# Two of six pairs of an encoder's down projection as seven block products, with corrections added to x by DMA

## The chip, the cores and the metric

The kernel runs on one core of a Trainium2 chip. The metric is the device time of one execution in microseconds (us), the median of several runs. A core has five engines, each with its own queue of instructions that it works through in order, and waits on semaphores: TensorE (PE in the profile), VectorE (DVE), ScalarE (ACT), GpSimd (POOL) and SyncE (SP), which here only issues loads. Sixteen DMA engines carry the transfers that SP and POOL issue.

## The reference

A trunk of two layers over 256 tokens of width 2048, all in float32. In each layer, with RMSNorm h = norm(x):

```python
proj = einsum('bsd,de->bse', h, w_in[l])          # q, k, v and a gated branch uv
a = dilated_attention(rope(q), rope(k), v)        # 8 heads of 128
g = chunked_spatial_gating(uv, ...)
x = x + einsum('bse,ed->bsd', concat(norm(a), norm(g)), w_out[l])
h = norm(x)
ff = silu(einsum(h, w_gate[l])) * einsum(h, w_up[l])   # 5632 columns
x = x + einsum('bsf,fd->bsd', ff, w_down[l])           # "down", 5632 rows to 2048 columns
```

A last RMSNorm follows. The change is in the last line, and in attention's tables (cosines, sines, mask).

## The kernel before

**Products.** A float32 product is made of three TensorE products (TERMS): each operand is split into a high part, which ScalarE rounds with a copy, and a low part, which VectorE gets by subtraction (`put_split2` for activations, `Group.split`, lines 861 and 862, for weights). high x high, high x low and low x high are summed in a PSUM bank.

**Groups.** The work is a row of 28 groups per layer. A group computes 256 tokens by two blocks of 512 columns, in four banks: v and z are the two blocks for the first 128 tokens, x and w for the second. The groups are, in order: 0 v, 1 and 2 qk (queries and keys), 3 gv, 4 u, 5 to 8 the output projection; then ff and down in four parts (FF_PARTS 3, 3, 3, 2): ff 9 to 11, down0 12 and 13, ff 14 to 16, down1 17 and 18, ff 19 to 21, down2 22 and 23, ff 24 and 25, down3 26 and 27. Layer 1 repeats them with numbers 28 higher. One ff group makes one block of 512 ff columns; a part's first down group adds the part's ff blocks, times their rows of w_down, to columns 0 to 1023 of x, its second to the rest.

**Pairs and slots.** The contraction goes by pairs of 128-row tiles. A plain pair is a slot "N" twice, once per half of the tokens, with 24 matmuls in all. In ff groups four of eight pairs already run as seven block products M1 to M7 (Strassen's scheme in Winograd's form), one slot each, in the order ORDER (FIRST for a layer's first). Their weights come as four quarters q11, q12, q22, q21. VectorE adds quarters in place (line 837), two further additions between quarters are accumulating DMAs from POOL's queue (line 841), and M1, M5, M6 and M7 leave corrections (lines 917 to 929) that VectorE adds to the banks at the end (line 937). Their activations need seven combinations for each pair (`sums`). Down groups before are plain: 6 pairs (4 in down3), 144 matmuls.

**Order.** The code is written slot by slot, and each engine takes its instructions in that order. Ahead of a slot's matmuls stand the loads due 5 slots later and the splits due 3 slots later (2 from an ff part's second group on); behind them one or two steps of side tasks (`spawn`, `run_side`): transposes, norms, gates, attention. `Ffn.turn` is such a task: it transposes a finished ff block in two steps (k = 0 and 2) and splits it. Loads need one of N_BIG buffers of 128x2048 ("big"), small tiles of 128x512 one of a ring of N_SX (`sx`), whose next user waits for the last user of the same buffer.

**Down's end.** When a bank of a down group closes, VectorE adds it to x in place (line 761).

## Time and profile before

| | us |
|---|---|
| median of three runs | 2159.31 (2158.47 to 2159.74) |
| profiled execution | 2160.09 |
| its span, first to last instruction | 2158.3 |
| TensorE busy | 2100.5, 9432 matmuls |
| VectorE busy | 1525.8 |
| ScalarE busy | 1072.7 |
| POOL busy | 117.7 |

The engines work beside each other, so busy times don't add up. The 1.8 us between span and execution lie around the instructions. In timelines each row has its start, its length and its count, and in square brackets the idle time of the engine ahead of it and who ended it.

### The profile page before, as it was taken

To read this page: it belongs to the slowest core of one execution; us is meant where nothing else is said; L and a number is where in the kernel's file an instruction comes from. 1 tells how busy PE (TensorE), PEld (TensorE's weight loads), DVE (VectorE), ACT (ScalarE), POOL (GpSimd) and SP (SyncE) were. 2 spreads that over 40 slices of the span, in tenths; PEclk is the share of its full clock that TensorE was granted. 3 is DMA by queue.
4 is the path that set the end of the run, shared out by engine and by line. 5 is a ranking of instruction groups with operands and counts; after the bars stand their busy time and mean duration, and the time that the engine had idled before them with its cause. 6 is when DMAs were issued, how large, how long until landed. Compare 5 with 4: busy or idle time off the path is not lost.

```text
span 2158.3 us, 23529 instructions
## 1 busy us (share of the span) xinstructions
PE 2100.5 (97%) x9432; PEld 1725.6 (80%) x9432; DVE 1525.8 (71%) x1388; ACT 1072.7 (50%) x1153; POOL 117.7 (5%) x108
## 2 busy tenths in 40 slices
PE   8999999999999999999999999999999999999997
PEld 7888887788888878888788788877888788788885
DVE  5577656886687588668655766668847875886684
ACT  6445545554455355445553555455534553554453
POOL 0220000000000000000002200000000000000000
PEclk9999999999999999999999999999999999999999
DMA  8444554676776667667544355556766665776772
GB/s 339 175 145 171 186 204 158 213 249 223 241 243 195 234 214 232 216 222 262 198 178 174 127 189 185 195 160 237 235 241 226 215 234 196 228 251 224 241 244 78
DMA packets 65134, 451.96 MB, mean 209 GB/s; under 512 B 7296, under 2 KB 7296, under 8 KB 11264
## 3 DMA queue, kind: packets, MB, share of 16 engines
q1 hardware_dynamic: 58688, 404.31, 50.1%
q0 software_dynamic: 6336, 46.14, 10.9%
q8 instruction: 74, 1.21, 0.2%
q14 instruction: 36, 0.29, 0.0%
HBM read 402.19 MB, written 2.10 MB: 187 GB/s over the span
## 4 chain that ended last, share of the span: by engine, by line
PE 50%; DVE 5%; issue 2%; ACT 2%; DMA 1%; DVEq 0%; POOLq 0%; POOL 0%; ACTq 0%
PE mm_v L884 12%; PE mm_z L884 11%; PE mm_x L884 11%; PE mm_w L884 10%; PE mm L884 5%; DVE lo_M L862 2%; DMA raw_q<-raw_q 1%; ACT hi_M L861 1%; DVE lo L862 1%; PE tpf L265 1%; DVE hl L862 0%; PE sp L449 0%; PE tpn_n L265 0%; DVE m L937 0%; PE op L489 0%
## 5 line engine op out<-in xcount | busy, mean ns | idle before, releaser
L862 DVE TENSOR_TENSOR hl<-raw,hl 128x1024 fp32r<-128x1024 f32 (+1 forms) x402 | 478.9, 1240 | 65.3 <-ACT hl L861 63.5
L861 ACT ACTIVATE hl<-raw 128x1024 fp32r<-128x1024 f32 (+1 forms) x402 | 399.6, 1048 | 129.2 <-PE mm_w L884 80.7
L862 DVE TENSOR_TENSOR lo_M<-raw_q,hi_M 128x2048 fp32r<-128x2048 f32 x154 | 348.8, 2287 | 77.3 <-ACT hi_M L861 72.5
L861 ACT ACTIVATE hi_M<-raw_q 128x2048 fp32r<-128x2048 f32 x154 | 287.3, 1910 | 108.2 <-DMA raw_q<-raw_q 82.6
L884 PE MATMUL mm<-hi_M,h_n 128*128 128x512 f32 x704 | 235.5, 395 | 8.2 <-ACT h_n L255 4.1
L862 DVE TENSOR_TENSOR lo<-raw,hi 128x2048 fp32r<-128x2048 f32 x88 | 201.1, 2285 | 41.9 <-ACT hi L861 31.5
L861 ACT ACTIVATE hi<-raw 128x2048 fp32r<-128x2048 f32 x88 | 167.1, 1907 | 54.4 <-PE mm_w L884 43.0
L884 PEld LDWEIGHTS mm<-hi_M,h_n 128*128 128x128 f32 x704 | 132.7, 189 | 38.0 <-DVE h_n L257 6.4
L884 PE MATMUL mm_v<-hl,ff 128*128 128x512 f32 x528 | 136.3, 392 | 2.7 <-ACT ff L234 2.7
L884 PE MATMUL mm<-lo_M,h_n 128*128 128x512 f32 x352 | 138.0, 392 | 0.0
L884 PE MATMUL mm_x<-hl,ff 128*128 128x512 f32 x528 | 134.9, 391 | 0.0
L884 PE MATMUL mm_z<-hl,ff 128*128 128x512 f32 x528 | 134.1, 389 | 0.0
L884 PE MATMUL mm_w<-hl,ff 128*128 128x512 f32 x528 | 134.1, 389 | 0.0
L884 PE MATMUL mm_v<-hi,hb_n 128*128 128x512 f32 x352 | 126.2, 399 | 0.0
L884 PE MATMUL mm_z<-hi,hb_n 128*128 128x512 f32 x352 | 124.3, 394 | 0.0
L884 PE MATMUL mm_x<-hi,hb_n 128*128 128x512 f32 x352 | 122.9, 390 | 0.0
L884 PE MATMUL mm_w<-hi,hb_n 128*128 128x512 f32 x352 | 122.7, 389 | 0.0
L884 PE MATMUL mm_v<-hl,h_n 128*128 128x512 f32 x420 | 113.7, 402 | 9.1 <-DVE hl L862 4.6
L884 PEld LDWEIGHTS mm_v<-hl,ff 128*128 128x128 f32 x528 | 98.0, 188 | 25.0 <-ACT ff L234 3.7
L884 PEld LDWEIGHTS mm_z<-hl,ff 128*128 128x128 f32 x528 | 99.1, 188 | 20.7
L884 PEld LDWEIGHTS mm_w<-hl,ff 128*128 128x128 f32 x528 | 99.1, 188 | 20.7
L884 PEld LDWEIGHTS mm_x<-hl,ff 128*128 128x128 f32 x528 | 98.5, 188 | 20.1
(207 smaller groups left out, 3368.4 us busy)
## 6 DMA issues: line engine op xcount, KB each, us to landing
raw<-in_w SPq DMA_DIRECT2D x287, 1024.0 KB, 4.9
raw_q<-in_w SPq DMA_DIRECT2D x88, 1024.0 KB, 6.8
raw_q<-raw_q POOLq DMA_DIRECT2D x44, 1024.0 KB, 7.8
xt<-in_x SPq DMA_DIRECT2D x4, 512.0 KB, 13.6
out<-xt SPq DMA_DIRECT2D x8, 256.0 KB, 3.1
...
raw<-in_w SPq DMA_DIRECT2D x4, 256.0 KB, 5.7
...
```

The lines of the kernel that those rows point to most:

```text
L265: nc.tensor.transpose(ps[:, j, t, :], src[:, t, (k + j) * P:(k + j + 1) * P], ident)
L861: nc.scalar.activation(out=hi[:, sl], in_=src[:, sl], func=AF.Copy)
L862: nc.vector.tensor_tensor(out=lo[:, sl], in0=src[:, sl], in1=hi[:, sl].bitcast(F32), op=ALU.subtract)
L884: nc.tensor.matmul(bank[0], lhsT=lhsT, rhs=rhs, start=bank[1], stop=stop)
```

## The change

Three things change.

**Products.** The down groups of parts 0 to 2 (twelve groups in both layers) run their first two pairs, which are the part's first ff block, as M1 to M7 in the order DOWN. The quarters come two to a buffer, `q11q12` and `q22q21`, each as one load of 1 MB; each product's high and low parts share one buffer. Per group VectorE adds quarters twice (128x1024, line 900 after) and POOL's queue twice (512 KB, line 903).

**Corrections.** ScalarE copies banks 1 and 5, VectorE makes the corrections (lines 1002, 1004, 1008, 1009 after), and `to_x` adds them to x with four accumulating DMAs of 256 KB from POOL's queue (line 989): v after M1, z after M6, x and w after M7. VectorE then adds the banks to x as before (line 816), and waits for those DMAs, because both write the same tile of x.

**Fast blocks.** For ff blocks 0, 3 and 6 `Ffn.turn` no longer splits after each transpose. ScalarE copies the transposed tiles into a raw buffer, and `sums` makes the seven combinations of both pairs and splits them.

**Tables.** The attention tables, their mask and a sum leave the constant pool for a big buffer `cm` that a Mixer takes at its start and frees after attention; layer 1 loads them a second time. N_BIG goes from 17 to 18, N_SX from 8 to 7.

The core of the diff; left out are renamed uses of the tables, the selection of the pairs and the layout of the packed weights, which follows the order of the loads.

```diff
-FAST = {"ff": 4}
+FAST = {"ff": 4, **{f"down{i}": 2 for i, n in enumerate(FF_PARTS) if n == 3}}
...
 ORDER = ("N", "M1", "N", "M5", "M2", "N", "M6", "M3", "M7", "M4", "N")
+DOWN = ("M1", "N", "M5", "N", "M2", "M6", "N", "M3", "M7", "M4", "N")
...
 LOADS = {"M1": ("q11", "q12"), "M5": ("q22",), "M2": ("q21",)}
+LOADS2 = {"M1": ("q11q12",), "M5": ("q22q21",)}
 CH = 4 * NB
-N_BIG = 17
-N_SX = 8
+N_BIG = 18
+N_SX = 7
...
 )
+FAST_BLOCKS = [sum(FF_PARTS[:i]) for i in range(len(FF_PARTS)) if FAST.get(f"down{i}")]
...
             for m in range(2):
-                yield (l, f"down{i}", m, j0 * NB, 2 * nj, 0,
+                yield (l, f"down{i}", m, j0 * NB, 2 * nj, FAST.get(f"down{i}", 0),
...
             j0 += nj
-def _order(idx, pairs, fast):
+def _order(what, idx, pairs, fast):
...
         return pairs * ("N",)
+    if what != "ff":
+        return DOWN
     return ORDER if idx else FIRST
+def _first(what, pairs, fast):
+    return pairs - fast if what == "ff" else 0
...
     colt = cpool.tile([P, DEPTH * (GC + NG)], F32, name="colt")
-    cst = cpool.tile([P, 2, NT, HD], F32, name="cst")
-    mskt = cpool.tile([P, NT, SEQ], F32, name="mskt")
...
         nc.vector.tensor_tensor(out=lo, in0=src, in1=hi.bitcast(F32), op=ALU.subtract)
-    def sums(raw, n, dst):
+    def sums(raw, n, dsts):
...
         src = r[:, :, 0:7, :].rearrange("p j f q -> p j (f q)")
-        hi, lo = (dst.rearrange("p (j h z) -> p j h z", h=2, z=7 * P)[:, :, i] for i in range(2))
-        nc.scalar.activation(out=hi, in_=src, func=AF.Copy)
+        per = n // len(dsts)
+        parts = []
+        for i, dst in enumerate(dsts):
+            z = dst.rearrange("p (j h z) -> p j h z", h=2, z=7 * P)
+            parts.append((z[:, :, 0], z[:, :, 1], src[:, i * per:(i + 1) * per]))
+        for hi, _, of in parts:
+            nc.scalar.activation(out=hi, in_=of, func=AF.Copy)
         yield 1
-        nc.vector.tensor_tensor(out=lo, in0=src, in1=hi.bitcast(F32), op=ALU.subtract)
+        for hi, lo, of in parts:
+            nc.vector.tensor_tensor(out=lo, in0=of, in1=hi.bitcast(F32), op=ALU.subtract)
...
             self.ra = self.rg = None
-            self.s2 = s2p.tile([P, SEQ], F32, tag="s2a", name=f"s2a_{l}", bufs=1)
+            self.cm = Big(f"cm_{l}")
+            self.cst = self.cm.t[:, :NB].rearrange("p (i t d) -> p i t d", i=2, t=NT)
+            self.mskt = self.cm.t[:, NB:2 * NB]
+            self.s2 = self.cm.t[:, 2 * NB:2 * NB + SEQ]
+            nc.sync.dma_start(out=self.cst, in_=cs)
+            nc.sync.dma_start(out=self.mskt, in_=msk.rearrange("p t k -> p (t k)"))
...
                     )
+                self.cm.free()
...
     class Ffn:
         def __init__(self, l, norm):
             self.l, self.norm = l, norm
-            self.blocks = {}
+            self.blocks, self.pairs = {}, {}
...
         def turn(self, m, ff, own):
-            self.blocks[m] = KTiles(f"ff_{self.l}_{m}")
+            fast = m in FAST_BLOCKS
+            if not fast:
+                self.blocks[m] = KTiles(f"ff_{self.l}_{m}")
+            else:
+                raw = Big(f"fr_{self.l}_{m}")
+                r = raw.view("p (j f q) -> p j f q", j=2, f=8)
...
                         own[0].free()
-                put_split2(self.blocks[m], k, ps.rearrange("p j t q -> p j (t q)"))
+                if fast:
+                    nc.scalar.activation(out=r[:, k // 2, 0:8:7, :], in_=ps[:, 0], func=AF.Copy)
+                    nc.scalar.activation(out=r[:, k // 2, 1:3, :], in_=ps[:, 1], func=AF.Copy)
+                else:
+                    put_split2(self.blocks[m], k, ps.rearrange("p j t q -> p j (t q)"))
+            if fast:
+                pair = [Big(f"ff_{self.l}_{m}_{i}", F32R) for i in range(2)]
+                yield from sums(raw, 2, [b.t[:, :14 * P] for b in pair])
+                self.pairs[m] = pair
+        def free(self, m):
+            for b in self.pairs[m] if m in FAST_BLOCKS else [self.blocks[m]]:
+                b.free()
+        def form(self, p):
+            m = p // 2
+            force(lambda: m in self.pairs)
+            v = self.pairs[m][p % 2].t[:, :14 * P].rearrange("p (h f q) -> p h f q", h=2, f=7)
+            return lambda hl, f: v[:, hl, FORMS[f], :]
...
     def before(l, what, idx):
         nonlocal final
-        if what == "v":
+        if what == "v" and l:
...
         return norms["n1", l].normal(p)
+    def form(l, what, p):
+        if what == "ff":
+            return norms["n2", l].form(p)
+        return ffns[l].form(sum(FF_PARTS[:int(what[4:])]) * 2 + p)
...
                 return [slot[0]]
-            return [slot[1]] if self.fast else [(slot[1], kk) for kk in range(2)]
+            return [slot[1]] if self.fast and not self.small else [(slot[1], kk) for kk in range(2)]
...
                 else:
-                    for q in LOADS.get(slot[0], ()):
-                        yield q, self.fast * NB, i
+                    for q in (LOADS2 if self.small else LOADS).get(slot[0], ()):
+                        yield q, 2 * NB * len(q) // 3 if self.small else self.fast * NB, i
...
             self.raw[key] = b
+        def block(self, q):
+            for key, b in self.raw.items():
+                if b.t is not None and isinstance(key, str) and q in key:
+                    c = key.index(q) // 3 * self.fast * NB
+                    return b.t[:, c:c + self.fast * NB]
         def add(self, to, of):
-            cols = self.fast * NB
-            a, b = (self.raw[q].t[:, :cols] for q in (to, of))
-            nc.vector.tensor_tensor(out=a, in0=a, in1=b, op=ALU.add)
+            nc.vector.tensor_tensor(out=self.block(to), in0=self.block(to), in1=self.block(of), op=ALU.add)
         def add_dma(self, to, of):
-            cols = self.fast * NB
-            nc.gpsimd.dma_start(out=self.raw[to].t[:, :cols], in_=self.raw[of].t[:, :cols], accum_op=ALU.add)
+            nc.gpsimd.dma_start(out=self.block(to), in_=self.block(of), accum_op=ALU.add)
         def need(self, key):
-            return 1 if isinstance(key, tuple) else 2
+            return 1 if isinstance(key, tuple) or self.small else 2
...
                 q = {"M1": "q11", "M5": "q11", "M6": "q11", "M2": "q21", "M4": "q21", "M7": "q12", "M3": "q22"}
-                raw, cols = self.raw[q.get(key, key)], self.fast * NB if key in PRODUCT else CH
-                src = raw.t[:, :cols]
-                own = [Big(f"{z}_{self.g}_{key}", F32R) for z in ("hi", "lo")]
-                hi, lo = (z.t[:, :cols] for z in own)
+                if key in PRODUCT:
+                    src, cols = self.block(q[key]), self.fast * NB
+                    raw = next(b for z, b in self.raw.items() if isinstance(z, str) and q[key] in z)
+                else:
+                    raw, cols = self.raw[key], CH
+                    src = raw.t
+                if self.small:
+                    own = [Big(f"hl_{self.g}_{key}", F32R)]
+                    hi, lo = own[0].t[:, :cols], own[0].t[:, cols:]
+                else:
+                    own = [Big(f"{z}_{self.g}_{key}", F32R) for z in ("hi", "lo")]
+                    hi, lo = (z.t[:, :cols] for z in own)
...
                 self.add_dma("q21", "q11")
+            elif self.small and key in ("M6", "M3"):
+                pass
...
                 for p in range(self.fast):
-                    act = norms["n2", self.l].form(self.n - self.fast + p)
+                    act = form(self.l, self.what, self.fasts[p])
...
                         z.free()
+        def to_x(self, b):
+            if self.what != "ff":
+                t, n = next(k for k, v in BANK.items() if v == b)
+                nc.gpsimd.dma_start(out=xt[2 * self.idx + n][:, t, :], in_=self.copies[b], accum_op=ALU.add)
...
                     c["v"] = c[b]
+                    self.to_x("v")
...
                 nc.vector.tensor_tensor(out=c["z"], in0=c["5"], in1=c["x"], op=ALU.subtract)
+                self.to_x("z")
...
                 c["w"] = c["5"]
+                self.to_x("x")
+                self.to_x("w")
                 return
-            if self.fast and b == "w" and "w" not in c:
+            if self.what == "ff" and b == "w" and "w" not in c:
...
                 return
-            if b in c:
+            if b in c and self.what == "ff":
...
         nc.sync.dma_start(out=xt[b], in_=x[:, :, b * NB:(b + 1) * NB])
-    nc.sync.dma_start(out=cst, in_=cs)
-    nc.sync.dma_start(out=mskt, in_=msk)
+    mixers[0] = Mixer(0, norms["n1", 0])
...
```

**Down to ff.** VectorE before, at the end of down0's second group (13) and the start of ff group 14; `hl` and `lo` are the low parts of weights, `xt` is x, `mm` a bank:

```order
L862 TENSOR_TENSOR hl_13_5_0_3884<-raw_13_5_3850,hl_13_5_0_3884 128x1024
L862 TENSOR_TENSOR hl_13_5_1_3887<-raw_13_5_3850,hl_13_5_1_3887 128x1024
L862 TENSOR_TENSOR lo_14_0_3933<-raw_14_0_3882,hi_14_0_3932 128x2048
L761 TENSOR_TENSOR xt_2_99<-mm_13_v_3770,xt_2_99 128x512
L761 TENSOR_TENSOR xt_3_100<-mm_13_z_3771,xt_3_100 128x512
L761 TENSOR_TENSOR xt_2_99<-mm_13_x_3792,xt_2_99 128x512
L761 TENSOR_TENSOR xt_3_100<-mm_13_w_3793,xt_3_100 128x512
```

The same place after the change:

```order
L932 TENSOR_TENSOR hl_13_M4_3952<-raw_13_q22q21_3761,hl_13_M4_3952 128x1024
L932 TENSOR_TENSOR hl_13_5_0_3961<-raw_13_5_3918,hl_13_5_0_3961 128x1024
L932 TENSOR_TENSOR hl_13_5_1_3964<-raw_13_5_3918,hl_13_5_1_3964 128x1024
L1008 TENSOR_TENSOR m16_13_3913<-mm_13_7_3967,m16_13_3913 128x512
L1009 TENSOR_TENSOR m5_13_3861<-m5_13_3861,m16_13_3913 128x512
L932 TENSOR_TENSOR lo_14_0_3991<-raw_14_0_3950,hi_14_0_3990 128x2048
L816 TENSOR_TENSOR xt_2_99<-mm_13_v_3818,xt_2_99 128x512
L816 TENSOR_TENSOR xt_3_100<-mm_13_z_3819,xt_3_100 128x512
L816 TENSOR_TENSOR xt_2_99<-mm_13_x_3838,xt_2_99 128x512
L816 TENSOR_TENSOR xt_3_100<-mm_13_w_3839,xt_3_100 128x512
L932 TENSOR_TENSOR lo_14_M1_4025<-raw_14_q11_3978,hi_14_M1_4024 128x2048
L900 TENSOR_TENSOR raw_14_q11_3978<-raw_14_q11_3978,raw_14_q12_3980 128x2048
```

POOL's queue after, for group 13 (before, it held nothing between groups 11 and 14):

```order
L989 DMA xt_2_99<-m1_13_3810 128x512
L903 DMA raw_13_q11q12_3728<-raw_13_q22q21_3761 128x1024
L903 DMA raw_13_q22q21_3761<-raw_13_q11q12_3728 128x1024
L989 DMA xt_3_100<-m5_16_13_3915 128x512
L989 DMA xt_2_99<-m16_13_3913 128x512
L989 DMA xt_3_100<-m5_13_3861 128x512
```

VectorE's additions to x stay ahead of the split of M1; ahead of them now stand three product splits and two bank operations, and on POOL's queue the DMAs on which the additions wait.

**The turn.** ScalarE before, in ff group 15, where ff block 3 is turned; `tpf` is the transposed tile, `m5` the copy of bank 5:

```order
L234 ACTIVATE ff_0_3_4313<-tpf_0_3_0_4331 128x2x256
L861 ACTIVATE hi_15_2_4338<-raw_15_2_4278 128x2048
L917 ACTIVATE m5_15_4355<-mm_15_5_4342 128x512
L234 ACTIVATE ff_0_3_4313<-tpf_0_3_2_4357 128x2x256
L861 ACTIVATE hi_15_M6_4376<-raw_15_q11_4180 128x2048
```

ScalarE after, `fr` being the raw buffer:

```order
L675 ACTIVATE fr_0_3_4371<-tpf_0_3_0_4389 128x2x128
L676 ACTIVATE fr_0_3_4371<-tpf_0_3_0_4389 128x256
L931 ACTIVATE hi_15_2_4396<-raw_15_2_4336 128x2048
L995 ACTIVATE m5_15_4413<-mm_15_5_4400 128x512
L675 ACTIVATE fr_0_3_4371<-tpf_0_3_2_4415 128x2x128
L676 ACTIVATE fr_0_3_4371<-tpf_0_3_2_4415 128x256
L274 ACTIVATE ff_0_3_0_4422<-fr_0_3_4371 128x896
L274 ACTIVATE ff_0_3_1_4423<-fr_0_3_4371 128x896
L931 ACTIVATE hi_15_M6_4444<-raw_15_q11_4238 128x2048
```

VectorE before, at the same place:

```order
L235 TENSOR_TENSOR ff_0_3_4313<-tpf_0_3_0_4331,ff_0_3_4313 128x2x256
L862 TENSOR_TENSOR lo_15_2_4339<-raw_15_2_4278,hi_15_2_4338 128x2048
L235 TENSOR_TENSOR ff_0_3_4313<-tpf_0_3_2_4357,ff_0_3_4313 128x2x256
L862 TENSOR_TENSOR lo_15_M6_4377<-raw_15_q11_4180,hi_15_M6_4376 128x2048
L862 TENSOR_TENSOR lo_15_M3_4395<-raw_15_q22_4237,hi_15_M3_4394 128x2048
```

VectorE after:

```order
L932 TENSOR_TENSOR lo_15_2_4397<-raw_15_2_4336,hi_15_2_4396 128x2048
L266 TENSOR_TENSOR fr_0_3_4371<-fr_0_3_4371 128x2x128 x4
L277 TENSOR_TENSOR ff_0_3_0_4422<-fr_0_3_4371,ff_0_3_0_4422 128x896
L277 TENSOR_TENSOR ff_0_3_1_4423<-fr_0_3_4371,ff_0_3_1_4423 128x896
L932 TENSOR_TENSOR lo_15_M6_4445<-raw_15_q11_4238,hi_15_M6_4444 128x2048
```

The four sums and the two splits of the block now stand together between the second N pair's low part and M6's, and M6's high part stands behind two copies more on ScalarE.

**From qk to gv.** VectorE before, in layer 0, with the engines it waits for in brackets; `rb` is one half of the rotation (POOL makes the other, `ra`), `hl_3_1` and `hl_3_2` are gv's weights:

```order
L862 TENSOR_TENSOR hl_3_1_1_1133<-raw_3_1_1064,hl_3_1_1_1133 128x1024 [waits Activation_49]
L419 TENSOR_TENSOR rb_q_0_1_1_1169<-s_q_0_1_1_1142,cst_102 128x4x64 [waits Activation_49,Pool_49]
L419 TENSOR_TENSOR rb_q_0_1_1_1169<-s_q_0_1_1_1142,cst_102 128x4x64
L419 TENSOR_TENSOR rb_k_0_1_1_1174<-s_k_0_1_1_1150,cst_102 128x4x64 [waits DVE_49,Activation_49,Pool_49]
L419 TENSOR_TENSOR rb_k_0_1_1_1174<-s_k_0_1_1_1150,cst_102 128x4x64
L862 TENSOR_TENSOR hl_3_2_0_1180<-raw_3_2_1128,hl_3_2_0_1180 128x1024 [waits DMAHW1_49,Activation_49]
L862 TENSOR_TENSOR hl_3_2_1_1183<-raw_3_2_1128,hl_3_2_1_1183 128x1024 [waits PE_49,Activation_49]
```

After:

```order
L932 TENSOR_TENSOR hl_3_1_1_1131<-raw_3_1_1062,hl_3_1_1_1131 128x1024 [waits Activation_49]
L445 TENSOR_TENSOR rb_q_0_1_1_1167<-s_q_0_1_1_1140,cm_0_128 128x4x64 [waits PE_49,Activation_49]
L445 TENSOR_TENSOR rb_q_0_1_1_1167<-s_q_0_1_1_1140,cm_0_128 128x4x64
L445 TENSOR_TENSOR rb_k_0_1_1_1172<-s_k_0_1_1_1148,cm_0_128 128x4x64 [waits DVE_49,Activation_49,Pool_49]
L445 TENSOR_TENSOR rb_k_0_1_1_1172<-s_k_0_1_1_1148,cm_0_128 128x4x64
L932 TENSOR_TENSOR hl_3_2_0_1178<-raw_3_2_1126,hl_3_2_0_1178 128x1024 [waits DMAHW1_49,Activation_49]
L932 TENSOR_TENSOR hl_3_2_1_1181<-raw_3_2_1126,hl_3_2_1_1181 128x1024 [waits Activation_49]
```

The order is the same; the second `rb_q` waits for PE in place of Pool.

## Rows read from the trace of the kernel before

**Rows 1.** Page: busy time by engine, and the granted clock by slice.

```profile
PE 2100.5 (97%) x9432; PEld 1725.6 (80%) x9432; DVE 1525.8 (71%) x1388; ACT 1072.7 (50%) x1153; POOL 117.7 (5%) x108
...
PEclk9999999999999999999999999999999999999999
```

**Rows 2.** TensorE's timeline, down2's first group: start us, us, engine, line, operation.

```profile
878.85 1.52 PE L884 MATMUL mm_v<-hl,ff 128*128 128x512 f32 x6
880.21 1.52 PE L884 MATMUL mm_z<-hl,ff 128*128 128x512 f32 x6
```

**Rows 3.** Stretches from:to: busy PE, PEld, DVE, ACT, POOL; granted clock; DMA share; GB/s.

```profile
878.85:912.20 33.35, 33.35 (x152) 27.62 (x151) 20.21 (x21) 16.35 (x18) 0.00 (x0) 1.00 0.53 190
912.20:945.07 32.87, 32.87 (x146) 27.21 (x145) 15.50 (x15) 11.90 (x9) 0.00 (x0) 1.00 0.66 256
996.00:1040.00 44.00, 43.75 (x197) 36.24 (x198) 37.33 (x30) 25.49 (x22) 0.86 (x1) 1.00 0.78 241
```

**Rows 4.** Groups by line and shape, VectorE, then ScalarE: count, busy us, mean ns.

```profile
L862 DVE TENSOR_TENSOR hl<-raw,hl 128x1024 fp32r<-128x1024 f32 x398 | 476.3, 1245 | 62.4 <-ACT hl L861 60.7
...
L837 DVE TENSOR_TENSOR raw_q<-raw_q,raw_q 128x2048 f32<-128x2048 f32 x44 | 100.9, 2292 | 1.5
...
L252 DVE TENSOR_TENSOR hr_n<-hr_n 128x256 f32<-128x256 f32 x16 | 6.1, 421 | 4.0 <-ACT hr_n L329 3.9
...
L861 ACT ACTIVATE hl<-raw 128x1024 fp32r<-128x1024 f32 x398 | 397.0, 1053 | 126.4 <-PE mm_w L884 80.7 <-DMA raw<-in_w 36.4 <-DVE hl L862 8.3
...
L917 ACT ACTIVATE m<-mm 128x512 f32<-128x512 f32 x44 | 26.3, 598 | 165.0 <-PE mm L884 165.0
```

**Rows 5.** Page: software queue and transfers, us to landing; L841: issue ns, landing us.

```profile
q0 software_dynamic: 6336, 46.14, 10.9%
...
out<-xt SPq DMA_DIRECT2D x8, 256.0 KB, 3.1
...
L841 POOL DMA_DIRECT2D raw_q<-raw_q x44: 852/862/1045, 358.3 to 2073.5; - x44
...
DMA to landing us min/median/max: 6.9/7.8/12.9
```

**Rows 6.** VectorE, then TensorE, from down2's last bank into the next ff group.

```profile
945.27 0.69 DVE L761 TENSOR_TENSOR xt<-mm_w,xt 128x512 f32<-128x512 f32 x1 [0.67 <-PE mm_w L884]
...
950.41 2.28 DVE L862 TENSOR_TENSOR lo<-raw,hi 128x2048 fp32r<-128x2048 f32 x1
...
953.46 0.39 PE L884 MATMUL mm_v<-lo,hb_n 128*128 128x512 f32 x1
```

**Rows 7.** ScalarE, VectorE, TensorE in ff group 15, at the second transpose.

```profile
617.50 5.53 ACT L861 ACTIVATE hi_M<-raw_q 128x2048 fp32r<-128x2048 f32 x3
...
616.81 2.28 DVE L862 TENSOR_TENSOR lo<-raw,hi 128x2048 fp32r<-128x2048 f32 x1
...
619.61 6.68 DVE L862 TENSOR_TENSOR lo_M<-raw_q,hi_M 128x2048 fp32r<-128x2048 f32 x3
...
616.33 0.60 PE L265 MATMUL tpf<-ident,ffn 128*128 128x128 f32 x4
...
625.18 0.39 PE L884 MATMUL mm<-lo_M,h_n 128*128 128x512 f32 x1
```

**Rows 8.** VectorE, then TensorE, from the second qk group into gv, layer 0.

```profile
154.99 1.85 DVE L419 TENSOR_TENSOR rb_q<-s_q,cst 128x256 f32<-128x256 f32 x2
159.58 0.76 DVE L419 TENSOR_TENSOR rb_k<-s_k,cst 128x256 f32<-128x256 f32 x2 [2.74 <-POOL ra_q L421]
160.26 3.44 DVE L862 TENSOR_TENSOR hl<-raw,hl 128x1024 fp32r<-128x1024 f32 x2
...
153.83 0.60 PE L430 MATMUL tpr_q<-ident,ra_q 128*128 128x128 f32 x4
...
161.53 0.97 PE L884 MATMUL mm_v<-hl,h_n 128*128 128x512 f32 x3 [0.97 <-DVE hl L862]
163.76 1.00 PE L884 MATMUL mm_v<-hl,h_n 128*128 128x512 f32 x2 [1.26 <-DVE hl L862]
```

More of the change, by code (lines that the diff above doesn't have):

```diff
@@ L333, in block @@
             if fast:
-                yield from sums(raw, len(fast), self.hs[:, (fast[0] - self.slow) * 14 * P:(fast[-1] + 1 - self.slow) * 14 * P])
+                sl = slice((fast[0] - self.slow) * 14 * P, (fast[-1] + 1 - self.slow) * 14 * P)
+                yield from sums(raw, len(fast), [self.hs[:, sl]])
                 for p in fast:
@@ L729, in after @@
             for j in range(sum(FF_PARTS[:i]), sum(FF_PARTS[:i + 1])):
-                ffns[l].blocks[j].free()
+                ffns[l].free(j)
     def normal(l, what, p):
@@ L783, in __init__ @@
             self.banks, self.copies = {}, {}
-            rest = iter(range(self.n - self.fast))
+            f0 = _first(self.what, self.n, self.fast)
+            self.fasts = range(f0, f0 + self.fast)
+            rest = iter(p for p in range(self.n) if p not in self.fasts)
+            self.small = self.fast == 2
             self.slots = []
-            for m in _order(self.idx, self.n, self.fast):
+            for m in _order(self.what, self.idx, self.n, self.fast):
                 if m == "N":
@@ L1053, in _stream @@
     parts = []
-    for l, _, idx, row, pairs, fast, blocks in _groups():
+    for l, what, idx, row, pairs, fast, blocks in _groups():
         ab = [weights[name][l, row:row + pairs * 2 * P, c:c + NB].reshape(pairs, 2, P, NB) for name, c in blocks]
         z = np.stack(ab, 2)
-        rest = iter(z[:pairs - fast])
-        for m in _order(idx, pairs, fast):
+        f0 = _first(what, pairs, fast)
+        rest = iter([z[p] for p in range(pairs) if not f0 <= p < f0 + fast])
+        for m in _order(what, idx, pairs, fast):
             if m == "N":
                 parts.append(next(rest).transpose(2, 0, 1, 3).ravel())
-            for q in LOADS.get(m, ()):
-                parts.append(z[pairs - fast:, int(q[1]) - 1, int(q[2]) - 1].transpose(1, 0, 2).ravel())
+            for q in (LOADS2 if fast == 2 else LOADS).get(m, ()):
+                c = [z[f0:f0 + fast, int(q[i + 1]) - 1, int(q[i + 2]) - 1] for i in range(0, len(q), 3)]
+                parts.append(np.concatenate(c).transpose(1, 0, 2).ravel())
     return np.concatenate(parts)
```

6 lines of the change are left out of this document (3 added, 3 removed).

## The prediction

> **What bounds the kernel now.** I read the page first: TensorE is busy 97% of the span and its granted clock is in the top tenth in all forty slices [rows 1], so time leaves this kernel by fewer matmuls or fewer TensorE waits, and by nothing else. Then I read TensorE's timeline in a down group: packs of six matmuls start 1.36 us apart, 226.7 ns each, and no row there names a wait [rows 2]. Next the stretches by engine [rows 3]: in the two groups of down2 TensorE is busy all of 33.35 and 32.87 us while VectorE works 20.21 and 15.50 of them; in the denser ff stretch VectorE works 37.33 of 44.00 and the DMA engines 78%. The price of each operation comes from the groups by line [rows 4] and the DMA rows [rows 5]. Last I followed, instruction by instruction, the three places where the order changes: the end of a down group [rows 6], the ff group that turns a fast block [rows 7], the step from qk to gv [rows 8]. The profiled run took 2160.09 us, 0.78 more than the median of 2159.31, so I make the sum from 2160.09 and take 0.78 off at the end.
>
> **1. Matmuls removed.** In each of twelve down groups two pairs of 24 matmuls become seven products of 6: 138 in place of 144. The shapes stay as they are, 128 rows by 512. That is 72 matmuls, and in the unbroken rhythm of [rows 2] 72 x 0.2267 = 16.3 us, all of it on the path as long as the weights' splits come in time. **Term: -16.3.**
>
> **2. Is what hides it still wide enough?** VectorE gains per group three half splits (7 products for 4 halves) at 1.245, two sums of 128x1024 of a resident block, and four bank operations of the shape of line 761's, 0.69 [rows 6]. The sums have no row of their own; half of the 128x2048 sum's 2.292 is 1.15, the split of the same shape 1.245; I take 1.2. Sum 3.7 + 2.4 + 2.8 = 8.9 us. So a part's first group goes from 20.2 to 29.1 of 32.0 us, its second from 15.5 to 24.4 of 31.5. ScalarE gains 3 x 1.053 + 2 x 0.6 = 4.4 us and stays near two thirds. I walked the new queues with these durations: each split ends 1 to 4 us before TensorE asks, the last N pair's second half with about 1. Cost 0; were each first group late by 2 us, six of them would cost 12.
>
> The DMA engines are the thinner cover. The software queue took 10.9% of 2158.3 us for 44 accumulating adds of 1 MB, 5.35 us of all sixteen engines for one [rows 5]. A down group gets 2 MB of these adds (two of 512 KB, four of 256 KB), so 10.7 us more. In the two groups of down2 the engines worked 0.53 x 33.35 + 0.66 x 32.87 = 39.4 us; with 21.4 more that is 60.8 of 63.5, against at most 0.78 in the dense stretches shown [rows 3]. Weight loads keep their size and number, so they should still land, but each transfer waits longer for an engine.
>
> **3. VectorE waits for the additions to x.** VectorE adds the banks to x as before, but only behind the DMAs. The late ones are x and w, issued after M7. Counted from M7's end: VectorE's two bank operations end at 0.7 and 1.4; the issues on the POOL queue cost 0.86 each [rows 5], so x goes out at 0.8 and w at 1.66; TensorE has M4 and the last N pair, 1.36 + 5.44 = 6.8 us, still to do. Before, VectorE added w as the bank closed, then split M1, added, and split the next N pair, done at 952.69, 0.77 us before TensorE's use at 953.46 [rows 6]. So a landing time up to 6.8 + 0.77 - 1.66 = 5.9 us is free, and each us beyond is lost, at six places. Between the two groups of a part the next splits are shorter and I find up to 8.3 us free.
>
> A 256 KB accumulating add is not in the trace. Nearest: a plain 256 KB store, 3.1 us, and the 1 MB accumulating add, 7.8 in the median, 12.9 at worst [rows 5]. In engine time it needs a quarter of 5.35, some 4 us less than the large one, which puts it near 4 in an easy stretch and, with the engines as full as in step 2, at 4 to 6. I take 5 and allow 2 us in all for stragglers. **Term: +2** (0 to 1.9 x 6 = 11.4 at 7.8). By the Trainium skill, "DMA: Bandwidth & Descriptors", section "Anatomy of one DMA", a transfer issued from GpSimd costs about 2.0 us and bytes over 436 GB/s; an estimate by it is 2.6 us here, and the term would be 0. For the 1 MB add that formula makes 4.4 where this trace shows 7.8, so the trace decides.
>
> **4. Turning a fast block.** In groups 10, 15 and 20 and their twins of layer 1, two transposes of the first ff block were each followed by a ScalarE copy and a VectorE subtraction. Now each is followed by two ScalarE copies of 128x256, and after the second come four VectorE sums (0.421 each), two ScalarE copies of 128x896 (0.95, a little less than the 1.053 for 1024 columns [rows 4]) and two subtractions, all queued ahead of the split of M6. Walk group 15 [rows 7]: the second N pair's low part, begun behind the longer first copies at 616.5, ends at 618.8; the sums end at 620.5, the copies at 622.4, M6's high part (1.84, a third of 5.53) at 624.2, its low part (2.28) at 626.5. TensorE wants it for M6's second matmul, at 625.18. Before, it was ready at 621.9. So a stall of 1.3, with the hand-overs between the engines 1.4, and six of these: **+8.4** (0 if the copies overlap more than I assume; 2.5 each, 15, if VectorE falls behind as well). M3 and M7 have the time that TensorE loses, and no second stall follows.
>
> **5. One ring buffer fewer in the mixer.** Before, VectorE's rb_k of the second token tile stood 2.74 us waiting for POOL's ra_q, and behind it the split that TensorE waits for twice, 0.97 and 1.26 us, at the start of gv in each layer [rows 8]. With seven buffers the ring is dealt out otherwise: rb_q waits for TensorE's transpose, which is over at 154.4, before rb_q's turn at 155.0; rb_k waits for POOL's first product and no longer for its sum. It can then go at 156.9, the split at about 158. I keep 0.4 of the 2.23. **Term: 2 x -1.8 = -3.6** (0 to -4.5; POOL works beside DVE's splits there, two in 3.44 against 1.245 each elsewhere, so a little may come back).
>
> **6. The rest.** The tables' second load, the eighteenth big buffer, and the extra POOL issues, which have an empty queue behind them outside the mixer (POOL is busy 5%): 0, within 2 either way.
>
> Sum: 2160.1 - 16.3 + 2 + 8.4 - 3.6 = 2150.6, less 0.8: **2149.8 us**.
>
> **Rivals.**
> *The turn is absorbed*: the copies run ahead and M6 is not late. 8.4 less: about 2141. For it: ScalarE works 25 of 44 us in such a stretch [rows 3]. Against: everything stands in one chain of two engines, and M6's split is behind it.
>
> *The accumulating DMAs become the bound* (slower). Place: the w addition before the first ff group of a part, six times, and from 8.3 us on the six between the groups as well. Price: beyond 5.9 us, 6 for each us. At 7.8 the result is 2149.8 - 2 + 11.4 = 2159.2, the whole gain gone; it decides from about 8.5, where it reads slower; at the 12.9 seen for the large adds, 6 x 7.0 + 6 x 4.6 = 70, some 2218. For it: sixteen engines filled to 0.96. Against: the large adds need four times the engine time. In the mixer VectorE and POOL slow each other, the pair of splits at 3.44 [rows 8]; beside it, POOL's 44 issues take 0.852 to 1.045 us [rows 5] in ff groups, where VectorE works 85% [rows 3]. [...]
>
> *VectorE is full in the first down groups*: the splits fall 1 to 2 us behind in six groups, 6 to 12 us back, 2156 to 2162. For: 91% busy. Against: its work is spread and begins a group ahead.
>
> *Loads come late*: a fast group holds two resident blocks of weights and a fast turn three big buffers, so with one more of them loads may start later in ff groups. 5 to 10 us, 2155 to 2160. If the products did not replace the pairs, the count would stay at 9432 and the time with it; I fold that in here.
>
> **How the numbers follow.** My sum 0.46 (own range 2145 to 2155); turn absorbed 0.13; DMAs the bound 0.18; VectorE full 0.14; loads 0.09. About 0.2%, 4.3 us, is what can be told from no change. Faster, below 2155: 0.44 + 0.13 + 0.03 + 0.06 + 0.03 = 0.69. Same: 0.02 + 0.05 + 0.06 + 0.05 = 0.18. Slower, above 2163.6: 0.10 + 0.02 + 0.01 = 0.13. The range runs from 2139 (terms 1 and 5 in full, little else) to 2163 (DMAs at about 8 us, or VectorE full with a turn of 2); it leaves out most of the DMA case beyond 8.5 and the best of the absorbed turn.
>
> **What would show it.** After: 9360 matmuls; down groups at 31.3 us with packs of six still 1.36 us apart (step 1), no wait inside (step 2); DMA share there 0.9 or more; the 256 KB adds landing below 6 us, and VectorE's x and w additions ended by TensorE, not by a DMA (step 3); six TensorE waits of about 1.4 us for lo_M in M6 of the ff groups (step 4); the 0.97 and 1.26 at gv gone (step 5). I am wrong if x additions wait for DMA with TensorE idle behind them, if the down groups keep 32.7 us, or if new waits for raw<-in_w stand on the path.

## The result

The changed kernel takes 2194.97 us (median of four runs, 2191.5 to 2197.15), the kernel before 2159.52 on the same chips. The ratio is 1.0165, 95% interval 1.0152 to 1.0177: 1.65% slower. The forecast was 2149.8, with a range of 2139 to 2163, so it is wrong in sign and the time lies far outside the range.

### The profile page after: what moved, and what is told of

It is laid out like the page before. It is cut to its first block, busy times and chain, and to the rows that moved or that the text cites. A ratio compares the mean times of both kernels' runs of the same rounds, so it can differ in the third digit from the quotient of the medians.

```text
span 2193.9 us, 23948 instructions
## 1 busy us (share of the span) xinstructions
PE 2102.0 (96%) x9360; PEld 1717.5 (78%) x9360; DVE 1644.6 (75%) x1520; ACT 1129.0 (51%) x1237; POOL 181.9 (8%) x180
## 3 DMA queue, kind: packets, MB, share of 16 engines
q0 software_dynamic: 16704, 71.31, 17.3%
## 4 chain that ended last, share of the span: by engine, by line
PE 68%; DVE 14%; issue 8%; DMA 5%; ACT 4%; POOL 1%; DVEq 0%; SPq 0%; POOLq 0%; ACTq 0%
PE mm_v L956 15%; PE mm_z L956 15%; PE mm_x L956 14%; PE mm_w L956 12%; PE mm L956 9%; DVE lo_M L932 5%; DMA xt<-m 3%; DVE lo L932 3%; ACT hi_M L931 2%; DMA raw_q<-raw_q 2%; DVE hl L932 2%; DVE rb_q L445 1%; DVE rb_k L445 1%; PE tpf L285 1%; PE op L515 1%
## 5 line engine op out<-in xcount | busy, mean ns | idle before, releaser
L932 DVE TENSOR_TENSOR hl<-raw,hl 128x1024 fp32r<-128x1024 f32 (+1 forms) x354 | 424.2, 1243 | 54.7 <-ACT hl L931 53.2
L931 ACT ACTIVATE hl<-raw 128x1024 fp32r<-128x1024 f32 (+1 forms) x354 | 351.8, 1048 | 72.6 <-DMA raw<-in_w 39.4
L932 DVE TENSOR_TENSOR lo<-raw,hi 128x2048 fp32r<-128x2048 f32 x88 | 201.1, 2286 | 12.7 <-ACT hi L931 12.6
L931 ACT ACTIVATE hi<-raw 128x2048 fp32r<-128x2048 f32 x88 | 166.5, 1907 | 37.0 <-DMA raw<-in_w 24.4
L995 ACT ACTIVATE m<-mm 128x512 f32<-128x512 f32 x68 | 40.6, 596 | 240.4 <-PE mm L956 238.3
L903 POOL DMA_DIRECT2D raw_q<-raw_q x44 | 38.2, 868 | 867.9 <-DVE raw_q L900 515.1
L956 PE MATMUL mm_z<-hl,h_n 128*128 128x512 f32 x420 | 109.2, 396 | 0.0
L956 PE MATMUL mm_x<-hl,h_n 128*128 128x512 f32 x420 | 109.1, 395 | 0.0
L956 PE MATMUL mm_w<-hl,h_n 128*128 128x512 f32 x420 | 107.0, 390 | 0.0
L956 PE MATMUL mm_v<-hl,ff 128*128 128x512 f32 x384 | 99.6, 392 | 2.9 <-ACT ff L248 2.8
L900 DVE TENSOR_TENSOR raw_q<-raw_q,raw_q 128x2048 f32<-128x2048 f32 x44 | 100.8, 2292 | 1.5
L956 PEld LDWEIGHTS mm_v<-hl,h_n 128*128 128x128 f32 x420 | 76.8, 190 | 27.9 <-DVE hl L932 8.1
```

The costliest lines, as they stand in the source:

```text
L900: nc.vector.tensor_tensor(out=self.block(to), in0=self.block(to), in1=self.block(of), op=ALU.add)
L903: nc.gpsimd.dma_start(out=self.block(to), in_=self.block(of), accum_op=ALU.add)
L931: nc.scalar.activation(out=hi[:, sl], in_=src[:, sl], func=AF.Copy)
L932: nc.vector.tensor_tensor(out=lo[:, sl], in0=src[:, sl], in1=hi[:, sl].bitcast(F32), op=ALU.subtract)
L956: nc.tensor.matmul(bank[0], lhsT=lhsT, rhs=rhs, start=bank[1], stop=stop)
L995: nc.scalar.activation(out=c[b], in_=ps, func=AF.Copy)
```

## The profile after

The page: busy time by engine, then the two DMA queues (packets, MB, share of sixteen engines). They answer to [rows 1] and to the first of [rows 5].

```profile
PE 2102.0 (96%) x9360; PEld 1717.5 (78%) x9360; DVE 1644.6 (75%) x1520; ACT 1129.0 (51%) x1237; POOL 181.9 (8%) x180
...
q1 hardware_dynamic: 58976, 404.83, 48.7%
q0 software_dynamic: 16704, 71.31, 17.3%
```

72 matmuls are gone, 9360 in place of 9432, but TensorE's busy time rose by 1.5 us and the span by 35.6. The software queue takes 17.3% in place of 10.9%. Two sizes on this page look as foreseen and are not the cause: the matmuls went, and the added DMA time, some 144 us of all sixteen engines, is near the 128 that were worked out.

To see where the time went, I took the start of each group's first matmul from TensorE's timeline of both kernels and summed the groups' lengths by their kind:

| groups | before, us | after, us | difference |
|---|---|---|---|
| 12 down groups of parts 0 to 2 | 397.4 | 381.7 | -15.6 |
| 6 ff groups right behind such a part (14, 19, 24 and twins) | 252.4 | 295.0 | +42.6 |
| 6 ff groups that turn a fast block (10, 15, 20 and twins) | 266.7 | 272.0 | +5.3 |
| 6 ff groups after those (11, 16, 21 and twins) | 257.6 | 261.2 | +3.6 |
| gv of both layers | 112.0 | 110.1 | -1.9 |
| all others | 851.6 | 852.2 | +0.6 |

The differences, taken before rounding, add up to 34.6 us; one more us lies ahead of the first matmul. One line of the table holds more than the whole loss. The stretches of down2's two groups and of the ff group behind them (24), columns as in [rows 3]; the last row is a piece of ff group 14:

```profile
890.85:923.10 32.25, 32.25 (x147) 26.70 (x147) 26.91 (x29) 17.46 (x20) 4.34 (x5) 1.00 0.84 249
923.10:954.38 31.28, 31.28 (x139) 25.90 (x138) 23.20 (x23) 18.45 (x17) 5.22 (x6) 1.00 0.94 303
954.38:1002.66 48.28, 43.73 (x181) 34.62 (x180) 35.69 (x23) 18.60 (x13) 1.72 (x2) 0.96 0.78 261
565.60:568.90 3.30, 3.30 (x9) 2.58 (x8) 3.30 (x2) 0.00 (x0) 0.86 (x1) 0.50 0.00 0
```

And that ff group in the kernel before:

```profile
945.07:987.14 42.07, 41.11 (x181) 33.71 (x180) 35.00 (x22) 18.72 (x13) 1.72 (x2) 1.00 0.78 250
```

The down groups are full: TensorE is busy 32.25 of 32.25 and 31.28 of 31.28 us, at the full clock, while the DMA engines work 84 and 94%. Then the ff group needs 48.28 us where it needed 42.07. It idles for 4.55 us where before it idled for 0.96. Behind that its clock is down, 0.96 of full in the mean, with stretches like the last row, where the granted clock is 0.50 (1.2 in place of 2.4 GHz) while TensorE is busy all 3.30 us. Step 3 below tells what that cost.

What TensorE waits for (us in total, times, longest):

```profile
PE mm L956 <- DVE lo_M L932: 14.1, 12, 1.6
PE mm L956 <- DVE xt L816: 13.7, 6, 3.0
...
PE mm_w L956 <- DVE xt L816: 1.4, 4, 0.7
```

None of the three stands in the trace of before. Six of the first twelve, 9.5 us, are this: lo_M of M1 is split behind the additions to x. The other six are those of step 4.

The end of group 13 and the start of ff group 14, VectorE (start, us; in brackets idle time and who ended it). It answers to the first row of [rows 6]:

```profile
547.73 0.69 DVE L1008 TENSOR_TENSOR m<-mm,m 128x512 f32<-128x512 f32 x1 [1.07 <-PE mm L956]
548.46 0.69 DVE L1009 TENSOR_TENSOR m<-m,m 128x512 f32<-128x512 f32 x1
549.07 2.29 DVE L932 TENSOR_TENSOR lo<-raw,hi 128x2048 fp32r<-128x2048 f32 x1
551.27 0.69 DVE L816 TENSOR_TENSOR xt<-mm_v,xt 128x512 f32<-128x512 f32 x1
551.87 0.68 DVE L816 TENSOR_TENSOR xt<-mm_z,xt 128x512 f32<-128x512 f32 x1
558.03 0.69 DVE L816 TENSOR_TENSOR xt<-mm_x,xt 128x512 f32<-128x512 f32 x1 [5.48 <-DMA xt<-m]
561.79 0.69 DVE L816 TENSOR_TENSOR xt<-mm_w,xt 128x512 f32<-128x512 f32 x1 [3.07 <-DMA xt<-m]
562.40 2.28 DVE L932 TENSOR_TENSOR lo_M<-raw_q,hi_M 128x2048 fp32r<-128x2048 f32 x1
```

POOL's issue of x and w in the same place, and the landing of these two:

```profile
548.72 1.75 POOL L989 DMA_DIRECT2D xt<-m  x2 [6.57 <-DVE m L1008]
...
DMA to landing us min/median/max: 9.2/10.7/12.3
```

TensorE, in M1 of group 14:

```profile
562.63 0.47 PE L956 MATMUL mm<-hi_M,h_n 128*128 128x512 f32 x1 [2.19 <-DVE xt L816]
564.74 0.51 PE L956 MATMUL mm<-lo_M,h_n 128*128 128x512 f32 x1 [1.64 <-DVE lo_M L932]
```

Read these from the top. M7's bank operations end at 549.1. POOL issues x at 548.72 and w at 549.45. VectorE adds v and z, then stands 5.48 us for x's DMA and, after that addition, 3.07 us for w's. They landed 9.2 and 12.3 us after issue, where 5.9 was worked out as free. Behind the additions stand M1's low part, which begins at 562.40 and not where TensorE could use it, and the banks: TensorE waits 2.19 us for a bank and 1.64 for lo_M. Then its clock is down for 3.4 us.

## Experiments

All times are set against runs of the kernel before on the same chip, 2158.8 to 2159.3 us.

**1. VectorE adds x and w itself, in a part's second group only.**

```diff
-nc.gpsimd.dma_start(out=xt[2 * self.idx + n][:, t, :], in_=self.copies[b], accum_op=ALU.add)
+to = xt[2 * self.idx + n][:, t, :]
+if self.idx and b in "xw":
+    nc.vector.tensor_tensor(out=to, in0=self.copies[b], in1=to, op=ALU.add)
+else:
+    nc.gpsimd.dma_start(out=to, in_=self.copies[b], accum_op=ALU.add)
```

> The changed kernel, but in the second down group of each part VectorE adds the corrections of x and w to x itself (two more 128x512 additions, 0.69 us each, six groups); the other corrections stay accumulating DMAs. Theory A (the ff group behind a part is late because VectorE stands at the additions to x until the DMAs of x and w land, 9 and 12 us after issue, and TensorE's clock is halved after the idle time): the six ff groups behind a part fall from 48.3 to 50.4 us back to about 42.1, 42 us in all, so 2151 to 2155 us. Rival B (the accumulating DMAs' traffic delays the weights of these ff groups): two thirds of the loss stays, since four of eight DMAs of a part remain and the weights come as before, 2175 to 2190 us.

Measured: 2151.47 us (2150.27 to 2153.64), ratio to before 0.9966 (0.9952 to 0.9980). The six ff groups take 252.4 us, as in the kernel before. The ff group 14 in this kernel, TensorE at the full clock:

```profile
550.00:592.00 42.00, 41.04 (x181) 33.66 (x180) 35.95 (x23) 19.58 (x13) 1.72 (x2) 1.00 0.83 281
```

Twelve of the 48 DMAs into x carried the whole loss of 43 us. This version beats both kernels.

**2. All DMAs kept, the wait for two taken away.** x's and w's corrections of a part's second group go into two dead tiles, so the result lacks them.

```diff
 to = xt[2 * self.idx + n][:, t, :]
+if self.idx and b in "xw":
+    to = self.copies["vz"["xw".index(b)]]
 nc.gpsimd.dma_start(out=to, in_=self.copies[b], accum_op=ALU.add)
```

> The changed kernel with all its DMAs, but the x and w corrections of a part's second group go into two small tiles that nobody reads any more, in place of x (so these corrections are left out of the result). The traffic is that of the changed kernel to the byte, only the wait of VectorE's additions to x is gone. Theory A (the wait): 2150 to 2155 us, and the DMAs still land 9 and 12 us after issue. Rival B (the traffic): time stays above 2180 us.

Measured: 2156.15 us (one run); the six ff groups 254.8. The landing of the two in the same place:

```profile
DMA to landing us min/median/max: 9.3/10.9/12.4
```

They land as late as before, 8.3 to 12.9 us after issue at the six places, and five of the six ff groups take the 42.1 us of the kernel before, as nobody waits. So it is the wait, not the traffic. In group 52 2.4 us are left: there TensorE waits 1.82 us for a lo_M whose quarter comes by a 1 MB accumulating DMA that landed 12.1 us after issue. The changed kernel has the same 1.82 us in that group, so about 2 of its 42.6 us are not the wait for x and w. Why it delays this group alone was not followed.

**3. Why they land late: loads written later.** The ff group's loads are written three slots ahead in place of five.

```diff
-        return 0
+        return -2 if gr.what == "ff" and groups[gr.g - 1].small else 0
...
```

> The changed kernel, but the weight loads of the ff group behind each of the three parts are written two slots later, 3 instead of 5 slots ahead. Theory A2 (x and w land late because they are queued behind a burst of six or seven 1 MB loads issued in the last 12 us before): with fewer loads ahead of them they land sooner, about 5 to 8 us after issue in place of 9.2 and 12.2, and the six groups lose 1 to 4 us each in place of 7; the time falls to 2160 to 2185 unless the weights themselves are late. Rival C (256 KB accumulating DMAs land late there for another reason, such as VectorE keeping GpSimd from writing descriptors while it splits): landing stays at 9 and 12 us.

Measured: 2196.73 us (one run), x and w in group 13 landing 9.0 and 12.1 us after issue. Time and landings stayed, but this settles nothing. The loads of 536.9 to 548.4 in the changed kernel went out at 538.0 to 549.6, each 0.7 to 4.6 us later, and x and w, issued at 548.6 and 549.3, still met three of them each. SP stands for buffers there, 10.0 us for TensorE's mm_w alone, so a load goes out when its buffer comes free, and the row's place moves it little. The edit did not do what it was made for.

**4. Loads made to follow.** Of the ff group behind a part every load but the first waits until VectorE has added x and w: VectorE touches the buffer of the second (q11) behind those additions, and SP's queue stands. These loads and their splits are written at the slot that uses them.

```diff
+    def behind(gr, key):
+        return gr.what == "ff" and gr.g and groups[gr.g - 1].small and key != 0
...
+                if key == "q11" and groups[self.g - 1].small:
+                    nc.vector.memset(b.t[:, :1], 0.0)
                 nc.sync.dma_start(out=dst, in_=src)
...
-        [(s - LA_LOAD - early(gr), 0, i) for i, (s, gr, *_) in enumerate(loads) if i >= KD // KR]
+        [(s - LA_LOAD * (not behind(gr, key)), 0, i) for i, (s, gr, key, *_) in enumerate(loads) if i >= KD // KR]
...
```

> The changed kernel, but in the ff group behind each of the three parts every weight load but the first is issued only after VectorE has added x and w (the next load's buffer is touched by VectorE behind those additions, and SP's queue waits for it). These loads are then late for TensorE, so the kernel is slower than the changed one, 2230 to 2500 us; what is to be read is the landing of the x and w corrections and VectorE's wait for them. Theory A2 (they land late because 1 MB weight loads are under way at their issue: 3.3 to 4.9 us with one of them, 9 to 12.8 with four): with one or none under way they land 3 to 6 us after issue, and VectorE's additions of x and w wait for TensorE's banks and not for a DMA. Rival C (VectorE's work, or the place itself): they still land after 9 and 12 us and VectorE waits 5 and 3 us for them.

Measured: 2333.29 us (one run), as the late loads make it. x and w in the same place, and VectorE's additions there:

```profile
DMA to landing us min/median/max: 3.3/3.7/4.1
```

```profile
552.94 0.68 DVE L816 TENSOR_TENSOR xt<-mm_v,xt 128x512 f32<-128x512 f32 x1
553.54 0.68 DVE L816 TENSOR_TENSOR xt<-mm_z,xt 128x512 f32<-128x512 f32 x1
554.85 0.69 DVE L816 TENSOR_TENSOR xt<-mm_x,xt 128x512 f32<-128x512 f32 x1 [0.62 <-PE mm_x L958]
556.21 0.69 DVE L816 TENSOR_TENSOR xt<-mm_w,xt 128x512 f32<-128x512 f32 x1 [0.67 <-PE mm_w L958]
```

Without those loads x and w land after 3.3 and 4.1 us, at all six places, and VectorE's additions are ended by TensorE's banks, 1.36 us apart, as in the kernel before. The queue of weight loads is the cause. The changed kernel's own 48 landings say the same: sorted by the number of 1 MB loads under way at the issue, the median is 3.9 us with one (20 DMAs), 6.1 with two (13), 9.2 with three (7) and 12.1 with four (8). All twelve at the end of a part met three or four. VectorE's work does not hold them up: it was busy for 85% or more of the time during the twelve landings here, and for 84 to 89% during the twelve late ones of experiment 2, where it did not wait for them.

SP's issues of weight loads (issue ns, first and last start) in the last 11 us of group 13 and, in the kernel before, in the same stretch:

```profile
L889 SPq DMA_DIRECT2D raw_q<-in_w x3: 327/328/328, 543.3 to 548.4; - x3
L889 SPq DMA_DIRECT2D raw<-in_w x2: 328/328/328, 544.3 to 551.4; - x2
```

```profile
L831 SPq DMA_DIRECT2D raw_q<-in_w x1: 328/328/328, 545.9 to 545.9; - x1
L831 SPq EVENT_SEMAPHORE  x1: 17/17/17, 546.3 to 546.3; - x1
L831 SPq DMA_DIRECT2D raw<-in_w x1: 328/328/328, 556.1 to 556.1; - x1
```

Five loads of 1 MB go out from 543.3 on, where the kernel before issues one at 545.9 (and one at 545.2, just ahead of this stretch) and the next at 556.1.

**5. More time in front of the wait.** The order of a down group's products is changed so that M7 stands one N pair earlier.

```diff
-DOWN = ("M1", "N", "M5", "N", "M2", "M6", "N", "M3", "M7", "M4", "N")
+DOWN = ("M1", "N", "M5", "N", "M2", "M6", "M3", "M7", "N", "M4", "N")
```

> The changed kernel with all DMAs and waits, but the products of a down group in the order M1 N M5 N M2 M6 M3 M7 N M4 N: one N pair (5.44 us) more stands between the issue of x's and w's corrections and the end of the group. Theory A: the landing time that costs nothing grows from 5.9 to 11.3 us; x (9.2) is hidden and w (12.2) by all but 1 us, so the ff groups behind a part lose 0 to 2 us each in place of 7, and TensorE's clock stays up: 2152 to 2164 us. If the DMAs land later by as much, because they then meet the next group's loads as before, the time stays above 2185.

Measured: 2179.25 us (2177.49 to 2180.25), ratio 1.0094 (1.0079 to 1.0109), between the two expectations and outside the first. VectorE at the end of group 13, M7's bank operation, then the additions of x and w:

```profile
545.75 0.68 DVE L1008 TENSOR_TENSOR m<-mm,m 128x512 f32<-128x512 f32 x1
...
558.24 0.69 DVE L816 TENSOR_TENSOR xt<-mm_x,xt 128x512 f32<-128x512 f32 x1 [2.71 <-DMA xt<-m]
562.04 0.69 DVE L816 TENSOR_TENSOR xt<-mm_w,xt 128x512 f32<-128x512 f32 x1 [3.11 <-DMA xt<-m]
```

The ff groups behind a part lose 12.7 us in place of 42.6. So cover helps, but the landing grew too, to 10.4 to 11.4 us for x and 13.5 to 14.5 for w, with z, x and w issued within 4 us behind each other, and the down groups lost the 15 us they had gained, since M6, M3 and M7 now follow each other and wait for VectorE.

**6. All four corrections on VectorE.** In `to_x` the addition of experiment 1 without its condition.

> The changed kernel with all four corrections of every down group added to x by VectorE, no DMA into x: four more 128x512 additions (0.69 us each) in each of twelve groups, 29.1 + 2.8 = 31.9 of 32.0 us in a part's first groups by the sum of the prediction. If VectorE's time there counts, the first groups lose 1 us or more each and the kernel takes 2155 to 2162 us. If that work lies beside TensorE after all and only the waits on DMAs cost, it is within 2 us of the run with two of four on VectorE, 2151.5.

Measured: 2154.03 us (2151.42 to 2155.58), ratio 0.9978 (0.9968 to 0.9987). That is between the two expectations, 2.6 us more than with two of four on VectorE, on another chip and with intervals that overlap. The down groups take 382.9 against 381.7 us. What was 31.9 of 32.0 us by my sum is 28.4 of 32.2 in down2's first group, so VectorE was not full there, and nothing costs 1 us a group.

**7. The turn, three slots later**, on top of experiment 1:

```diff
+                yield 3
                 pair = [Big(f"ff_{self.l}_{m}_{i}", F32R) for i in range(2)]
                 yield from sums(raw, 2, [b.t[:, :14 * P] for b in pair])
```

> VectorE adds the x and w corrections of a part's second group, as in the run with those two on VectorE, and the fast block's sums and splits stand three slots later, behind the splits of M6 and M3 on ScalarE and VectorE. If the waits of 0.8 us for M6's low part in groups 10, 15, 20 and their twins are due to those sums, these six groups come back to the times of the kernel before within 0.3 us (they are 0.4 to 1.1 longer now) and the kernel takes 2145 to 2149 us. If VectorE is simply full in these ff groups, the wait moves to M7 or M4 of the same group and the time stays within 2 us of 2151.5.

Measured: 2168.09 us, ratio 1.0045 (1.0029 to 1.0062): slower than experiment 1 by 17. In group 15 the wait for M6 is gone, and two larger ones have come, for the bank that VectorE's operation on M6 frees and for M4's low part:

```profile
632.53 0.47 PE L957 MATMUL mm<-hi_M,h_n 128*128 128x512 f32 x1 [1.73 <-DVE m L1007]
...
637.36 0.50 PE L957 MATMUL mm_x<-lo_M,h_n 128*128 128x512 f32 x1 [1.61 <-DVE lo_M L933]
```

The six groups take 289.1 us in place of 272.0. So work put between M3's and M7's splits costs each of these groups 2.9 us; the groups after them take 260.2 us as against 260.3.

**8. The turn spread out**, on top of experiment 1: the four sums stay, the two copies go behind the high part of M7, the two subtractions one by one behind M4's low part and into the next group.

```diff
...
+        if wait:
+            yield wait
         for hi, _, of in parts:
             nc.scalar.activation(out=hi, in_=of, func=AF.Copy)
-        yield 1
-        for hi, lo, of in parts:
+        yield 0 if wait else 1
+        for i, (hi, lo, of) in enumerate(parts):
+            if i and gap:
+                yield gap
...
```

The call gets wait=4, gap=3.

> VectorE adds x and w as in the run with those two on VectorE, the fast block's four sums stay where the change put them, but ScalarE's two copies stand behind the high part of M7 and VectorE's two subtractions one by one behind the low parts of M4 and later. If the wait for M6's low part comes from the copies ahead of its high part, as the prediction's walk has it, the six ff groups lose 0 to 0.4 us in place of 0.4 to 1.1 and the kernel takes 2146 to 2150 us. If VectorE has no room anywhere in these groups, the wait moves as it did when all was put three slots later, and the time is 2152 us or more.

Measured: 2146.99 us (2146.87 to 2148.56), ratio 0.9942 (0.9926 to 0.9959). The six groups take 266.0 us, those of the kernel before 266.7; the groups after them give back some (262.0 against 260.3). No wait of M6 for lo_M is left in them. This is the fastest version here.

**9. The ring alone.** The kernel before, N_SX 7 in place of 8.

> The kernel before, with seven small ring buffers in place of eight and nothing else. If the 1.7 us that the changed kernel gains in layer 0's gv group come from the ring, this kernel is 1 to 2.5 us faster than the kernel before, 2157 to 2158.5 us, with gv of layer 0 at 54.3 us in place of 56.0 and that of layer 1 within 0.3. If they come from the tables' new place, it is the same within 0.5 us.

Measured: 2159.17 us against 2159.02, ratio 0.9999 (0.9989 to 1.0008). The profile shows gv of layer 0 at 54.3 us in place of 56.0; the median shows no gain, though its interval would still hold one of 1.7 us.

## Why the prediction was wrong, step by step

**Step 1, matmuls: right.** Ten of the twelve down groups are shorter by 1.36 us to the hundredth and two, 17 and 45, by 1.01, together 15.6 for 16.3 predicted.

**Step 2, the cover: right in what it was asked.** No down group has a new wait of any size. VectorE worked 26.9 and 23.2 us in down2's groups where 29.1 and 24.4 were worked out, and the DMA share came to 0.84 and 0.94 where 0.96 over both was worked out. What I drew from the last number was too little: I asked whether the weights would still land, and they did.

**Step 3, the wait for x and w: this one failed, by its size.** The mechanism, the free time of 5.9 us and the six places are as written. The landing was put at 5 us, and over all 48 it is 5.6 in the median. But it is not one number. The two that matter are issued just when the next group's loads crowd in, and in group 13 they take 9.2 and 12.3. In all six w takes 11.9 to 12.8, and what lies beyond 5.9 adds up to 38.6 us where the term was +2; that was the slower rival, which I held to 0.18. I had reasoned from a transfer's size (a quarter of 1 MB) and from a mean DMA share, where the landing is set by what is queued ahead at the moment of the issue, up to four loads of 1 MB. Those loads were in reach of the prediction: SP issues when buffers come free, the new order held which buffers these are, and I used it to check the splits alone.

The clock was not in the sum at all, and it looks like a second piece. The mean granted clock of the changed kernel, then of the kernel before:

```profile
core 0: 2193.9 us, clock 0.986
```

```profile
core 0: 2158.3 us, clock 0.992
```

1.4% of 2193.9 us against 0.8% of 2158.3 are 31 and 17 us of full-speed work, so some 13 to 14 us more are lost at half clock. Stretches at 0.50 stand behind idle time in each of the six ff groups, 3.4 or 6.8 us each, 27.3 us in all; in experiment 1 they are gone. But most of this costs nothing, because another engine is later still. The chain of step 3 ends with the low part of the second N pair. In group 14 VectorE's split of it, then TensorE's use:

```profile
566.92 2.29 DVE L932 TENSOR_TENSOR lo<-raw,hi 128x2048 fp32r<-128x2048 f32 x1
...
569.27 0.50 PE L956 MATMUL mm_v<-lo,hb_n 128*128 128x512 f32 x1
```

At half clock TensorE comes 0.06 us after VectorE is done, and so it does in four of the six groups; at the full clock it would have stood and waited. In experiment 5 it does: the clock stays up in five of the six groups, and TensorE waits 1.5 us for this low part in each. In the two groups with 6.8 us at half clock TensorE comes 0.70 and 0.48 us after the split, so there the clock cost some 1 us in all. Up to this matmul the six groups lose 40.8 of their 42.6 us, close to the 38.6 of the step's own chain; the other 1.8 are group 52's (experiment 2).

The formula of the Trainium skill in "DMA: Bandwidth & Descriptors", section "Anatomy of one DMA", makes 2.6 us (an estimate); nearest to it is the 3.3 us of experiment 4, and the landings at a part's end are far from it.

**Step 4, the turn: right in mechanism, too large.** TensorE waits for M6's low part in all six groups, here in group 15:

```profile
630.29 0.50 PE L956 MATMUL mm<-lo_M,h_n 128*128 128x512 f32 x1 [0.77 <-DVE lo_M L932]
```

0.77 us where 1.4 was forecast; the six groups lose 5.3 us for 8.4. In this group VectorE stands 0.55 us for M6's high part, behind ScalarE's copies, and experiment 8, which moves the copies and the subtractions together, takes TensorE's wait away. Experiment 7 shows that the place matters by several us. Another 3.6 us appear in the groups after these six, where the step foresaw no second stall: in groups 11 and 21 TensorE waits 1.06 us for a low part for which it waited 0.56 before. What delays it was not followed.

**Step 5, the ring: wrong.** The second token tile's rb_k does go earlier, but VectorE's operations beside POOL's grew, rb_q from 1.85 [rows 8] to 2.94 us, and the splits end as late as before. VectorE in layer 1, then TensorE:

```profile
1239.23 2.94 DVE L445 TENSOR_TENSOR rb_q<-s_q,cm 128x256 f32<-128x256 f32 x2
1242.31 1.86 DVE L445 TENSOR_TENSOR rb_k<-s_k,cm 128x256 f32<-128x256 f32 x2
1244.09 3.43 DVE L932 TENSOR_TENSOR hl<-raw,hl 128x1024 fp32r<-128x1024 f32 x2
...
1245.35 0.96 PE L956 MATMUL mm_v<-hl,h_n 128*128 128x512 f32 x3 [0.71 <-DVE hl L932]
1247.57 0.73 PE L956 MATMUL mm_v<-hl,h_n 128*128 128x512 f32 x2 [1.26 <-DVE hl L932]
```

0.71 and 1.26 stand where 0.97 and 1.26 stood. I had priced the rotation at its old duration and kept the contention for the splits alone. The 1.7 us that layer 0's gv seemed to gain are a stretch at half clock that the profile of before has and that of after has not; the same window of layer 0 in both, before and then after:

```profile
164.60:167.80 3.20, 3.20 (x12) 2.51 (x11) 2.23 (x5) 2.40 (x4) 0.00 (x0) 0.55 0.00 0
```

```profile
164.60:167.80 3.20, 3.20 (x18) 2.64 (x17) 1.85 (x4) 2.65 (x5) 0.00 (x0) 1.00 0.01 3
```

Nothing ties this to the change. In the ten profiles with seven buffers gv has its two waits of 0.7 and 1.26 us each time, and the stretch at half clock follows them in 10 of 20 places: the group takes 55.8 us with it and 54.3 without, in either layer. With eight buffers there is one profile, with the stretch in both layers.

**Step 6: right**, the other groups differ by 0.6 us, and 1.0 us comes ahead of the first matmul. **The other rivals:** the turn absorbed and late loads did not come; VectorE full did not either, experiment 6.
